# The residual rows go to DRAM as two fp16 parts, and the experts' slots are transposed as fp16

## The chip, the cores and the metric

The kernel runs on one core of one Trainium2 chip. The engines named here are PE (TensorE, matrix products and transposes; its weight loads have a row PEld of their own), DVE (VectorE), ACT (ScalarE), POOL (GpSimd) and SP (SyncE, which here only issues DMAs). They run their own instruction streams and meet at semaphores. The metric is the device time of one execution in microseconds, as the median of several runs.

## The reference

Two layers work on one sequence of 512 rows of 1024 numbers. Each layer has three sub-layers, and each ends in a layer norm over the residual sum.

```python
def grouped_moe(x, w_router, b_router, w_gate, w_up, w_down):
    xt = x.reshape(B * S, D)
    scores = jax.nn.softmax((xt @ w_router + b_router).astype(jnp.float32), axis=-1)
    ...                     # best group of experts, then the two best experts in it
    for e in range(N_EXPERTS):
        h = jax.nn.silu(xt @ w_gate[e]) * (xt @ w_up[e])
        y = y + gate[:, e:e + 1] * (h @ w_down[e])

def reference(x, mem, ...):
    for l in range(DEPTH):
        ...                 # gated linear attention and spatial gating, output projection
        x = layer_norm(DN_ALPHA * x + h, ln_g[l, 0], ln_b[l, 0])
        h = mem_xattn(x, mem, wq_x[l], wk_x[l], wv_x[l], wo_x[l])
        x = layer_norm(DN_ALPHA * x + h, ln_g[l, 1], ln_b[l, 1])
        h = grouped_moe(x, w_router, b_router, w_gate[l], w_up[l], w_down[l])
        x = layer_norm(DN_ALPHA * x + h, ln_g[l, 2], ln_b[l, 2])
```

The change touches the third sub-layer, the grouped mixture of 16 experts, and how the rows of `x` come to it. All inputs and the output are fp32.

## The kernel before

Every fp32 matrix product is made of three fp16 products. A number is scaled and split into a high fp16 part and a low part (the rest, rounded to fp16), and `mm3` (L167 to L170) adds high x high, high x low and low x high in PSUM. The scale of the weights is 256, of the activations 16 (`SX`). A split is one ACT copy for the high part, followed by one DVE pass (`SCALAR_TENSOR_TENSOR`: scale, subtract the high part) for the low part: `split_ps` (L172 to L174) does it out of PSUM.

**The weights** come in units of 128 x 2048 fp32 (1 MiB) through `Feed` (L66 to L157). `fill` (L90 to L100) lets SP issue a load (L98) whenever a raw slot is free. `pump` splits the oldest loaded unit: ACT makes `whi` (L124), DVE makes `wlo` (L129). With `aside`, DVE is left out: ACT makes `whi`, scales the raw unit in place (L126), and POOL subtracts (L127). When a unit is split its raw slot's kind is appended to the queue `rawfree`, and `fill` takes slots from the front of that queue, so slots go round in the order in which splits free them. Four slots of kind "b" exist throughout. During the experts there are more: seven of kind "x" (`RAW_X`), two of kind "y", and in layer 1 one called "mem". In the last layer the last eight units may take only slots "b" and "mem" (`xend`, L876). An odd expert's last down unit (not that of expert 15) is not split but read by PE as raw fp32 (L1216), and frees its slot only then.

**Ahead of the experts** the output projection of the cross-attention runs over four tiles of 128 rows (tiles 0 to 3, order at L1083 to L1119). Each tile gets its residual sum (L337), its statistics (L290, L293; ACT L294, L296) and its layer norm (L300, L303), all on DVE in place in the tile's fp32 rows `xr`. Tile 3 does the norm in two halves. Then `x3T` (L931) sends the tile's rows to the DRAM array `xd` by a DMA on ACT's queue (L932), PE transposes the tile, and `split_ps` makes the fp16 parts `x` for the router. `logits` (L937, DVE L942) and `route` (from L965, with L967) choose the experts. Between the tiles stand weight splits set aside to POOL, two in each layer and a third in layer 0 (L1096, L1101, L1110).

**The experts** have 96 slots each. POOL gathers an expert's rows from `xd` with an indirect DMA (L1137) into one of three fp32 buffers, three experts ahead. `dispatch` (L1152) turns a buffer: eight fp32 transposes on PE into two PSUM banks, and per bank one split into `xgh` (ACT L173) and `xgl` (DVE L174), 384 columns each. `gate_up` (L1169) makes both products; ACT's SiLU (L1177) and DVE's product (L1178) make `h`. `hid` (L1198) splits `h` (ACT L1203, DVE L1204). `down` (L1230) is the down projection; ACT L1234 takes it out of PSUM and POOL scatters the rows to DRAM (L1143). One turn of the loop (L1329 to L1340) is, in the order of the code: `gate_up(e)`, `dispatch(e + 1)`, `hid(e)`, one weight split, the gather of expert e + 3, and `down(e - 1)`; each engine follows that order in its own stream.

Of the kernel before, what the change touches and what calls it, by code (L numbers as in the profile page):

```python
# [36 lines left out]
RAW_B, HL_B = 4, 4  # L37
RAW_X, HL_X, RAW_Y = 7, 1, 2
YEND = 4
# [5 lines left out]
def trunk_kernel(ctx, tc, units, xT, x, memT, alow, wa2, b_a, gn_g, w_sT, b_s, slnT,  # L45
# [12 lines left out]
    def nm(s):  # L58
        cnt[0] += 1
        return f"{s}_{cnt[0]}"  # L60

    def ps():
        return psp.tile([P, 512], F32, tag="b", name=nm("ps"))


    class Feed:  # L66
        def __init__(self):
            self.items = []
            self.raw = {}
            self.hl = {}  # L70
            self.nload = 0
            self.nsplit = 0
            self.rawfree = deque("b" * RAW_B)
            self.hlfree = deque("b" * HL_B)
            self.px = self.px2 = self.ph = None
            self.limit = 1 << 30
# [13 lines left out]
        def fill(self, eng=nc.sync):  # L90
            while self.nload < min(len(self.items), self.limit):
                k = self.slot(self.rawfree, self.nload)
                if k is None:
                    return
                src, _, _, cols = self.items[self.nload]
                pl, b = {"b": (ring, RAW_B), "x": (self.px, RAW_X), "y": (self.px2, RAW_Y), "mem": (cp, 1)}[k]
                t = pl.tile([P, 2048], F32, tag="mem" if k == "mem" else "raw", bufs=b, name=nm("raw"))
                eng.dma_start(t[:, :cols], src)  # L98
                self.raw[self.nload] = (t, k)
                self.nload += 1  # L100
# [109 lines left out]

    xd = dram.tile([S, D], F32, name="xd")
    y2 = dram.tile([2 * S, D], F32, name="y2")
# [214 lines left out]
    for l in range(DEPTH):  # L427
# [441 lines left out]
        with ExitStack() as ex:  # L869
# [5 lines left out]
            fin = l == DEPTH - 1  # L875
            feed.xend = {"h": u["end"], "x": u["end"] - (8 if fin else 0), "y": u["end"] - (8 if fin else YEND), "mem": u["end"]}  # L876
            feed.limit = u["end"] + 4
# [53 lines left out]
            def x3T(t):  # L931
                nc.scalar.dma_start(xd[t * P:(t + 1) * P, :], xr[t])  # L932
                x3hl = (ep if t % 2 else x3p).tile([P, 2, KT, P], F16, tag="xg2" if t % 2 else "x3", name=nm("x3"))
                x3[t] = (x3hl[:, 0], x3hl[:, 1])
                transpose_x(t, *x3[t])

            def logits(t):  # L937
# [175 lines left out]
            rows = cp.tile([P, 4, D], F32, tag="actA", name=nm("rows"))  # L1113
            xg32 = [rows[:, 0], rows[:, 1]]
            for g in xg32:
                pool.memset(g, 0.0)
            idle(6, 0, 0)
            logits(NT - 1)
            xg32.append(ep.tile([P, D], F32, tag="xg2", name=nm("xg2")))  # L1119
            pool.memset(xg32[2], 0.0)  # L1120
            x3c.__exit__(None, None, None)
# [30 lines left out]
            def dispatch(e):  # L1152
                g = xg32[e % 3]
                xgh = ep.tile([P, KT, CAP], F16, tag="xgh", name=nm("xgh"))
                xgl = ep.tile([P, KT, CAP], F16, tag="xgl", name=nm("xgl"))
                for hf in range(2):
                    p = ps()
                    for j in range(4):
                        k = 4 * hf + j
                        pe.transpose(p[:, j * CAP:(j + 1) * CAP], g[:CAP, k * P:(k + 1) * P], ident[:CAP, :CAP])  # L1160
                    split_ps(xgh[:, 4 * hf:4 * hf + 4].rearrange("p k c -> p (k c)"),
                             xgl[:, 4 * hf:4 * hf + 4].rearrange("p k c -> p (k c)"), p[:, :4 * CAP], SX)
                E[e] = {"xg": (xgh, xgl)}

            def fetch(e):
                if e < NE:
                    gather(xg32[e % 3], idxT[:, e:e + 1])

# [90 lines left out]
            def overflow(fp):  # L1259
                most = nc.values_load(cnti[0:1, NE:NE + 1], min_val=0, max_val=S)  # L1260
                with tc.If(most > CAP):  # L1261
                    off = fp.tile([P, 1], F32, name="off")
                    dve.memset(off, 0.0)
                    with tc.For_i(CAP, S, CAP) as first:
                        dve.tensor_scalar(off, off, float(CAP), None, op0=OP.add)
                        with tc.For_i(0, NE, 1) as e:
                            ce = nc.values_load(cnti[0:1, bass.ds(e, 1)], min_val=0, max_val=S)
                            with tc.If(ce > first):
# [13 lines left out]
                                row_of(pg[:, 1:4], 1, ix[:, 1:2], gf)  # L1282
                                gather(xg32[0], ix[:CAP, 0:1])
                                xg = fp.tile([P, KT, CAP], F32, name="xg")
                                for hf in range(2):
                                    p = ps()
                                    for j in range(4):
                                        k = 4 * hf + j
                                        pe.transpose(p[:, j * CAP:(j + 1) * CAP], xg32[0][:CAP, k * P:(k + 1) * P],
                                                     ident[:CAP, :CAP])  # L1290
                                    act.activation(xg[:, 4 * hf:4 * hf + 4].rearrange("p k c -> p (k c)"),
                                                   p[:, :4 * CAP], AF.Copy)

# [60 lines left out]
            if not fin:  # L1354
                ln_open()
                load_ln(l, 2)
                down(NE - 1)
                pxc.__exit__(None, None, None)
                phc.__exit__(None, None, None)
                with tc.tile_pool(name=f"ovf{l}", bufs=1, reuse_waits="tile") as fp:  # L1360
                    overflow(fp)
            else:

                pxc.__exit__(None, None, None)
                ln_open()
# [164 lines left out]
```

## Time and profile before

| | |
|---|---|
| median of 3 runs | 1277.48 us (1275.62 to 1279.99) |
| the profiled execution's own time | 1278.14 us |
| its span (first to last instruction) | 1276.5 us |
| PE busy | 1172.9 us (92%), 11218 instructions |
| DVE busy | 909.9 us (71%), 1066 instructions |
| ACT busy | 711.1 us (56%), 810 instructions |
| POOL busy | 234.5 us (18%), 193 instructions |
| mean DMA rate over the span | 247 GB/s |

The table is of one profiled execution. The shares are means over stages that differ much: the two expert loops lie at about 385 to 615 us and 1010 to 1235 us, where the weights stream in at about 418 GB/s; ahead of each is the stage with the output projection, the layer norm and the routing. A row of a timeline gives the start of an instruction, its duration and, in brackets, how long its engine stood idle before it and which instruction's end released it.

### The profile page before, as it was taken

The numbers are of one execution on the slowest core, as the hardware profiler recorded it, in microseconds if no ns is written. First come the engines' busy times: TensorE is split into PE (matmuls) and PEld (weight loads), VectorE is DVE, ScalarE is ACT, GpSimd is POOL, SyncE is SP. The second block draws the span as 40 slices with busy tenths as digits, with TensorE's granted clock in tenths as the row PEclk, the third lists the DMA queues.
The fourth block names the chain that finished last, engine by engine and source line by source line (L and its number), as shares of the span: only waits on it lengthen the run. The fifth ranks groups of instructions, "written<-read, shape, count | busy, mean of one in ns | idle before, by whom it ended". The sixth has DMA issues, their size and how long they took to land. (4 is left out here: it accounts for less than half of the span.)

```text
span 1276.5 us, 26079 instructions
## 1 busy us (share of the span) xinstructions
PE 1172.9 (92%) x11218; PEld 760.2 (60%) x11219; DVE 909.9 (71%) x1066; ACT 711.1 (56%) x810; POOL 234.5 (18%) x193
## 2 busy tenths in 40 slices
PE   7999999999979999999859999999999899999973
PEld 4455456454557777777635545444644777777751
DVE  3255875378579999999474275673857789999977
ACT  3435334345448888888443444232633588888863
POOL 3002000000231223321250003000003222223214
PEclk9999999999989999999979999999998899999996
DMA  9412225227569999999671230154374799999964
GB/s 361 163 67 99 99 77 188 99 99 292 220 226 371 419 418 418 419 417 405 233 273 79 99 133 34 67 215 181 112 312 139 274 389 419 417 419 419 373 241 180
DMA packets 54941, 314.76 MB, mean 247 GB/s; under 512 B 9310, under 2 KB 9406, under 8 KB 22561
## 3 DMA queue, kind: packets, MB, share of 16 engines
q1 hardware_dynamic: 42096, 279.99, 56.0%
q0 software_dynamic: 11568, 28.83, 6.3%
q10 hardware_dynamic: 1152, 4.19, 0.8%
q8 instruction: 90, 1.47, 0.5%
q14 instruction: 35, 0.28, 0.1%
HBM read 302.80 MB, written 22.68 MB: 255 GB/s over the span
## 5 line engine op out<-in xcount | busy, mean ns | idle before, releaser
L129 DVE SCALAR_TENSOR_TENSOR wlo<-raw,whi 128x2048 f16<-128x2048 f32 (+1 forms) x234 | 521.8, 2277 | 101.0 <-ACT whi L124 100.6
L124 ACT ACTIVATE whi<-raw 128x2048 f16<-128x2048 f32 (+1 forms) x239 | 440.9, 1894 | 32.9 <-DMA raw<-in_units 16.7
L170 PE MATMUL ps<-xgh,wlo 128*128 128x96 f16 x2048 | 270.4, 207 | 12.9 <-DVE wlo L129 12.9
L168 PE MATMUL ps<-xgh,whi 128*128 128x96 f16 x2048 | 270.3, 207 | 4.7 <-ACTq L1261 4.2
L169 PE MATMUL ps<-xgl,whi 128*128 128x96 f16 x2048 | 270.2, 207 | 1.1 <-DVE xgl L174 1.1
L170 PEld LDWEIGHTS <-wlo 128*128 128x128 f16 x2400 | 236.4, 98 | 50.7 <-DVE wlo L129 16.7
L168 PEld LDWEIGHTS <-whi 128*128 128x128 f16 x2400 | 236.5, 99 | 39.1 <-issue 6.0
L169 PEld LDWEIGHTS <-whi 128*128 128x128 f16 x2400 | 236.4, 99 | 38.2 <-issue 8.5
L1143 POOL DMA_INDIRECT y<-rows,idxR x31 | 71.4, 2303 | 340.8 <-ACT rows L1234 331.1
L168 PE MATMUL ps<-whi,xT 128*128 128x512 f16 (+1 forms) x256 | 92.6, 362 | 8.4 <-ACT whi L124 7.1
L170 PE MATMUL ps<-whi,xT 128*128 128x512 f16 (+1 forms) x256 | 92.4, 361 | 2.2 <-DVE xT L174 2.2
L169 PE MATMUL ps<-wlo,xT 128*128 128x512 f16 (+1 forms) x256 | 92.5, 361 | 1.7 <-DVE wlo L129 1.7
L168 PE MATMUL ps<-whi,hhl 128*96 128x512 f16 x200 | 75.9, 379 | 1.1 <-ACT hhl L1203 1.1
L169 PE MATMUL ps<-wlo,hhl 128*96 128x512 f16 x200 | 75.7, 379 | 0.9 <-DVE wlo L129 0.9
L170 PE MATMUL ps<-whi,hhl 128*96 128x512 f16 x200 | 75.8, 379 | 0.0
L294 ACT ACTIVATE lnmv<-lnmv,c_lneps 128x1 f32<-128x1 f32 x16 | 4.7, 295 | 110.0 <-DVE lnmv L293 110.0
L1203 ACT ACTIVATE hhl<-h 128x384 f16<-128x384 f32 x32 | 16.7, 523 | 74.9 <-DVE h L1178 74.8
L1216 PE MATMUL ps<-raw,h 128*96 128x512 f32 x112 | 50.3, 592 | 0.0
L169 PE MATMUL ps<-x2T,whi 128*128 128x512 f16 x128 | 48.5, 379 | 1.0 <-DVE x2T L174 1.0
L169 PE MATMUL ps<-wlo,mx 128*128 128x512 f16 x128 | 48.5, 379 | 0.4 <-DVE wlo L129 0.3
L1137 POOL DMA_INDIRECT rows<-xd,idxT x22 | 40.4, 1838 | 45.6 <-DVE wlo L129 11.1
L168 PE MATMUL ps<-x2T,whi 128*128 128x512 f16 x128 | 48.5, 379 | 0.0
(309 smaller groups left out, 2052.2 us busy)
## 6 DMA issues: line engine op xcount, KB each, us to landing
raw<-in_units SPq DMA_DIRECT2D x249, 1024.0 KB
xd<-xr ACTq DMA_DIRECT2D x8, 512.0 KB
ya<-y SPq DMA_DIRECT2D x8, 512.0 KB
yb<-y SPq DMA_DIRECT2D x8, 512.0 KB
y<-zr SPq DMA_DIRECT2D x1, 4096.0 KB
lng<-in_ln_g POOLq DMA_DIRECT2D x6, 512.0 KB, 5.3
lnb<-in_ln_b POOLq DMA_DIRECT2D x6, 512.0 KB, 7.1
raw<-in_xT SPq DMA_DIRECT2D x4, 512.0 KB
```

Source lines behind the costliest of these rows:

```text
L124: act.activation(dest[0], t[:, :cols], AF.Copy, scale=scale)
L129: dve.scalar_tensor_tensor(dest[1], t[:, :cols], scale, dest[0], op0=OP.mult, op1=OP.subtract)
L168: pe.matmul(o, lh, rh, start=first, stop=False)
L169: pe.matmul(o, lh, rl, start=False, stop=False)
L170: pe.matmul(o, ll, rh, start=False, stop=last)
L294: act.activation(mvt[:, 2:3], mvt[:, 1:2], AF.Ln, bias=c_lneps, scale=(ISC * ISC if scaled else 1.0))
L1137: pool.indirect_dma_start(out=dst[:idx.shape[0], :], out_offset=None, in_=xd[:], in_offset=bass.IndirectOffsetOnAxis(ap=idx, axis=0), boun ...
L1143: i = pool.indirect_dma_start(out=y2[:], out_offset=bass.IndirectOffsetOnAxis(ap=idx, axis=0), in_=src[:CAP, :], in_offset=None, bounds_ch ...
L1203: act.activation(f2(hh), h32, AF.Copy)
L1216: pe.matmul(p[:CAP, :], E[e]["h"][:, f * CAP:(f + 1) * CAP], mv(w, f), start=(f == 0), stop=(f == 3))
```

## The change

The DRAM array `xd` held a row as 1024 fp32 numbers; now it holds 2048 fp16 numbers, the row's high part and its low part, both already scaled by 16. `x3T(t)` makes these parts itself: after the transposes and splits of the tile, one ACT copy (high) and one DVE pass (low) over 1024 columns of `xr[t]` into a tile `xs` (two of them, in a pool of their own). The DMA of tile t - 1 is now issued at the start of `x3T(t)`, the last after `logits(3)`. The gathers bring both parts with the same number of bytes a row. `dispatch` turns sixteen fp16 blocks instead of eight fp32 ones, eight into each PSUM bank, and takes each bank out with one plain ACT copy of 768 columns; DVE takes no part. The transposes need an fp16 identity (one DVE cast in each layer). One of the seven raw slots "x" is given up for the tiles `xs` and comes back as a slot "z" when these are no longer needed. The overflow path, for experts with more than 96 rows, is changed in the same manner; it stands in a branch.

```diff
-RAW_X, HL_X, RAW_Y = 7, 1, 2
+RAW_X, HL_X, RAW_Y, RAW_Z = 6, 1, 2, 1
...
-                pl, b = {"b": (ring, RAW_B), "x": (self.px, RAW_X), "y": (self.px2, RAW_Y), "mem": (cp, 1)}[k]
+                pl, b = {"b": (ring, RAW_B), "x": (self.px, RAW_X), "y": (self.px2, RAW_Y), "z": (self.pz, RAW_Z), "mem": (cp, 1)}[k]
...
-    xd = dram.tile([S, D], F32, name="xd")
+
+    xd = dram.tile([S, 2 * D], F16, name="xd")
...
-            feed.xend = {"h": u["end"], "x": u["end"] - (8 if fin else 0), "y": u["end"] - (8 if fin else YEND), "mem": u["end"]}
+            xsc = tc.tile_pool(name=f"xs{l}", bufs=1, reuse_waits="tile")
+            xsp = xsc.__enter__()
+            feed.xend = {"h": u["end"], "z": u["end"] - (8 if fin else 0), "x": u["end"] - (8 if fin else 0), "y": u["end"] - (8 if fin else YEND), "mem": u["end"]}
...
             def x3T(t):
-                nc.scalar.dma_start(xd[t * P:(t + 1) * P, :], xr[t])
+                if t > 0:
+                    put(t - 1)
...
                 transpose_x(t, *x3[t])
+                xs[t] = xsp.tile([P, 2, D], F16, tag="xs", bufs=2, name=nm("xs"))
+                act.activation(xs[t][:, 0], xr[t], AF.Copy, scale=SX)
+                dve.scalar_tensor_tensor(xs[t][:, 1], xr[t], SX, xs[t][:, 0], op0=OP.mult, op1=OP.subtract)
+
+            xs = {}
+
+            def put(t):
+                nc.scalar.dma_start(xd[t * P:(t + 1) * P, :], xs[t].rearrange("p a d -> p (a d)"))
...
-            xg32 = [rows[:, 0], rows[:, 1]]
-            for g in xg32:
+            half = lambda v: v.bitcast(F16)
+            xg16 = [half(rows[:, 0]), half(rows[:, 1])]
+            for g in (rows[:, 0], rows[:, 1]):
                 pool.memset(g, 0.0)
+            id16 = ep.tile([P, CAP], F16, name="id16")
+            dve.tensor_copy(id16, ident[:, :CAP])
             idle(6, 0, 0)
             logits(NT - 1)
-            xg32.append(ep.tile([P, D], F32, tag="xg2", name=nm("xg2")))
-            pool.memset(xg32[2], 0.0)
+            put(NT - 1)
+            xsc.__exit__(None, None, None)
+            pzc = tc.tile_pool(name=f"pz{l}", bufs=1, reuse_waits="tile")
+            feed.pz = pzc.__enter__()
+            feed.rawfree.extend("z" * RAW_Z)
+            xg2 = ep.tile([P, D], F32, tag="xg2", name=nm("xg2"))
+            pool.memset(xg2, 0.0)
+            xg16.append(half(xg2))
...
             def dispatch(e):
-                g = xg32[e % 3]
-                xgh = ep.tile([P, KT, CAP], F16, tag="xgh", name=nm("xgh"))
-                xgl = ep.tile([P, KT, CAP], F16, tag="xgl", name=nm("xgl"))
+                E[e] = {"xg": []}
                 for hf in range(2):
-                    p = ps()
-                    for j in range(4):
-                        k = 4 * hf + j
-                        pe.transpose(p[:, j * CAP:(j + 1) * CAP], g[:CAP, k * P:(k + 1) * P], ident[:CAP, :CAP])
-                    split_ps(xgh[:, 4 * hf:4 * hf + 4].rearrange("p k c -> p (k c)"),
-                             xgl[:, 4 * hf:4 * hf + 4].rearrange("p k c -> p (k c)"), p[:, :4 * CAP], SX)
-                E[e] = {"xg": (xgh, xgl)}
+                    x16 = ep.tile([P, KT, CAP], F16, tag="xg" + "hl"[hf], name=nm("x16"))
+                    p = turned(xg16[e % 3], hf)
+                    act.activation(x16.rearrange("p k c -> p (k c)"), p, AF.Copy)
+                    E[e]["xg"].append(x16)
+
+            def turned(g, hf):
+
+                p = ps().bitcast(F16)
+                for k in range(KT):
+                    c = hf * D + k * P
+                    pe.transpose(p[:, k * CAP:(k + 1) * CAP], g[:CAP, c:c + P], id16[:CAP, :])
+                return p[:, :KT * CAP]
```

The lines move by the added code: L300 becomes L301, L303 L304, L337 L338, the logits' L942 L954, L967 L979, L1178 L1202, L1203 L1227, L1204 L1228, L1234 L1258. L942 is now the low part of `xs`, L941 its high part.

**DVE, between tiles 2 and 3 of layer 0.** `xr_87` and `xr_88` are the rows of tiles 2 and 3, `x_324` and `x_325` the fp16 parts of the transposed tile 2. Before:

```order
L337 SCALAR_TENSOR_TENSOR xr_88<-xr_88,ps_2694 128x512
L290 BN_STATS lnst_2778<-xr_88 128x6
L174 SCALAR_TENSOR_TENSOR x_324_2815<-ps_2816,x_324_2815 128x512
L174 SCALAR_TENSOR_TENSOR x_324_2815<-ps_2823,x_324_2815 128x512
L337 SCALAR_TENSOR_TENSOR xr_88<-xr_88,ps_2789 128x512
L290 BN_STATS lnst_2778<-xr_88 128x6
```

Now:

```order
L338 SCALAR_TENSOR_TENSOR xr_88<-xr_88,ps_2697 128x512
L291 BN_STATS lnst_2784<-xr_88 128x6
L174 SCALAR_TENSOR_TENSOR x_325_2821<-ps_2822,x_325_2821 128x512
L174 SCALAR_TENSOR_TENSOR x_325_2821<-ps_2829,x_325_2821 128x512
L942 SCALAR_TENSOR_TENSOR xs_2836<-xr_87,xs_2836 128x1024
L338 SCALAR_TENSOR_TENSOR xr_88<-xr_88,ps_2795 128x512
L291 BN_STATS lnst_2784<-xr_88 128x6
```

The pass L942 on tile 2's rows has come between tile 2's splits and the second half of tile 3's residual sum; tiles 0, 1 and 3 have the same pass behind their splits.

**DVE, one expert in layer 0's loop.** `h` is the expert's hidden product, `xgl` the low part of the next expert's rows, `hhl` the low part of `h`. Before:

```order
L129 SCALAR_TENSOR_TENSOR wlo_3785<-raw_3148,whi_3784 128x2048
L1178 SCALAR_TENSOR_TENSOR h_408_3673<-ps_3681,h_408_3673 128x384
L174 SCALAR_TENSOR_TENSOR xgl_3889<-ps_3890,xgh_3888 128x384
L174 SCALAR_TENSOR_TENSOR xgl_3889<-ps_3897,xgh_3888 128x384
L1204 TENSOR_TENSOR hhl_3904<-h_408_3673,hhl_3904 128x384
L129 SCALAR_TENSOR_TENSOR wlo_3908<-raw_3205,whi_3907 128x2048
L129 SCALAR_TENSOR_TENSOR wlo_3918<-raw_3259,whi_3917 128x2048
```

Now:

```order
L129 SCALAR_TENSOR_TENSOR wlo_3824<-raw_3175,whi_3823 128x2048
L1202 SCALAR_TENSOR_TENSOR h_412_3712<-ps_3720,h_412_3712 128x384
L1228 TENSOR_TENSOR hhl_3949<-h_412_3712,hhl_3949 128x384
L129 SCALAR_TENSOR_TENSOR wlo_3953<-raw_3232,whi_3952 128x2048
L129 SCALAR_TENSOR_TENSOR wlo_3963<-raw_3286,whi_3962 128x2048
```

The two passes for `xgl` between the product and the split of `h` are gone; the weight splits around them stand as they did.

**SP, the last loads of layer 1's weights.** Each row is a load of one unit; in brackets what SP waits for ahead of it: earlier DMAs (DMAHW), and the split (DVE) or the matrix product (PE) that frees the slot. Before:

```order
L98 DMA raw_14387<-in_units 128x2048 [waits DMAHW1_49,DVE_49]
L98 DMA raw_14397<-in_units 128x2048 [waits DMAHW2_49,DVE_49]
L98 DMA raw_14653<-in_units 128x2048 [waits DMAHW4_49,DMAHW3_49,DVE_49]
L98 DMA raw_14677<-in_units 128x2048 [waits DMAHW6_49,DVE_49]
L98 DMA raw_14755<-in_units 128x2048 [waits DMAHW5_49,DMAHW1_49,DVE_49]
L98 DMA raw_14809<-in_units 128x2048 [waits DMAHW2_49,DVE_49]
L98 DMA raw_14932<-in_units 128x2048 [waits DMAHW7_49,DMAHW3_49,DVE_49]
L98 DMA raw_14939<-in_units 128x2048 [waits DMAHW0_49,PE_49]
```

Now:

```order
L98 DMA raw_14491<-in_units 128x2048 [waits DMAHW1_49,DVE_49]
L98 DMA raw_14620<-in_units 128x2048 [waits DMAHW2_49,DVE_49]
L98 DMA raw_14630<-in_units 128x2048 [waits DMAHW3_49,DVE_49]
L98 DMA raw_14892<-in_units 128x2048 [waits DMAHW4_49,DVE_49]
L98 DMA raw_14916<-in_units 128x2048 [waits DMAHW6_49,DMAHW5_49,DVE_49]
L98 DMA raw_14994<-in_units 128x2048 [waits DMAHW1_49,DVE_49]
L98 DMA raw_15048<-in_units 128x2048 [waits DMAHW7_49,DMAHW2_49,DVE_49]
L98 DMA raw_15177<-in_units 128x2048 [waits DMAHW3_49,DMAHW0_49,DVE_49]
```

Before, the last load takes the slot of the raw unit that PE reads; now all eight take slots that a split frees.

## Rows read from the trace of the kernel before

**Rows 1.** Page, its first line (the span) and the row of its forty slices with the busy share of the core's 16 DMA engines in tenths.

```profile
span 1276.5 us, 26079 instructions
...
DMA  9412225227569999999671230154374799999964
```

**Rows 2.** Busy time of each engine in one stretch of layer 0's expert loop, 30.46 us long: from one scatter of an even expert to the next. Columns: the window, its length, PE, PEld, DVE, ACT and POOL busy us (instructions), granted clock, DMA share, GB/s.

```profile
430.46:460.92 30.46, 29.38 (x444) 23.45 (x444) 28.21 (x20) 25.39 (x24) 8.92 (x4) 1.00 1.02 418
```

**Rows 3.** Timeline of DVE in that stretch. Columns: start us, duration us (of a run of x instructions, together), engine, line, operation, out<-in, shape; in brackets the idle time before it and what released it.

```profile
442.13 0.55 DVE L1178 SCALAR_TENSOR_TENSOR h<-ps,h 128x384 f32<-128x384 f32 x1
442.60 1.01 DVE L174 SCALAR_TENSOR_TENSOR xgl<-ps,xgh 128x384 f16<-128x384 f32 x2
443.53 0.55 DVE L1204 TENSOR_TENSOR hhl<-h,hhl 128x384 f16<-128x384 f32 x1
445.07 4.49 DVE L129 SCALAR_TENSOR_TENSOR wlo<-raw,whi 128x2048 f16<-128x2048 f32 x2 [0.99 <-ACT whi L124]
```

**Rows 4.** Timeline of ACT in the same stretch.

```profile
439.30 0.85 ACT L173 ACTIVATE xgh<-ps 128x384 f16<-128x384 f32 x2
442.71 0.52 ACT L1203 ACTIVATE hhl<-h 128x384 f16<-128x384 f32 x1 [2.56 <-DVE h L1178]
443.14 3.69 ACT L124 ACTIVATE whi<-raw 128x2048 f16<-128x2048 f32 x2
```

**Rows 5.** Groups of instructions over the whole span, shapes kept apart. Columns: line, engine, operation, out<-in, shape, count | busy us together, mean ns of one | idle time before them and what ended most of it.

```profile
...
L124 ACT ACTIVATE whi<-raw 128x2048 f16<-128x2048 f32 x237 | 438.8, 1901 | 32.3 <-DMA raw<-in_units 16.2 <-PE ps L170 15.8 <-issue 0.2
...
L174 DVE SCALAR_TENSOR_TENSOR xgl<-ps,xgh 128x384 f16<-128x384 f32 x64 | 32.6, 548 | 8.0 <-ACT xgh L173 7.7
...
L173 ACT ACTIVATE xgh<-ps 128x384 f16<-128x384 f32 x64 | 27.6, 482 | 33.1 <-PE ps L1160 32.8
...
L129 DVE SCALAR_TENSOR_TENSOR xT<-raw,xT 128x1024 f16<-128x1024 f32 x4 | 4.9, 1225 | 9.3 <-ACT xT L124 9.3
```

**Rows 6.** Timeline of DVE ahead of layer 0's expert loop: the end of the output projection with its layer norms (L337, L300, L303), the splits of the transposed tiles (L174), and the first steps of the routing (L942, L967).

```profile
333.47 0.68 DVE L337 SCALAR_TENSOR_TENSOR xr<-xr,ps 128x512 f32<-128x512 f32 x1
...
336.53 0.69 DVE L337 SCALAR_TENSOR_TENSOR xr<-xr,ps 128x512 f32<-128x512 f32 x1 [1.66 <-PE ps L170]
...
343.16 1.29 DVE L174 SCALAR_TENSOR_TENSOR x<-ps,x 128x512 f16<-128x512 f32 x2 [0.92 <-ACT x L173]
344.37 0.68 DVE L337 SCALAR_TENSOR_TENSOR xr<-xr,ps 128x512 f32<-128x512 f32 x1
...
346.05 1.96 DVE L300 SCALAR_TENSOR_TENSOR xr<-xr,lnmv,lng 128x512 f32<-128x512 f32 x2
347.94 1.40 DVE L303 SCALAR_TENSOR_TENSOR xr<-xr,lnmv,lnb 128x512 f32<-128x512 f32 x2
...
352.73 0.17 DVE L942 SCALAR_TENSOR_TENSOR scs<-ps,scs 128x16 f32<-128x16 f32 x1 [0.51 <-PE ps L170]
...
353.19 1.46 DVE L967 TENSOR_TENSOR scs<-scs,cr 128x64 f32<-128x64 f32 x1
```

**Rows 7.** Timeline of POOL in the same stretch: the subtractions of the weight splits that are set aside.

```profile
331.88 4.08 POOL L127 TENSOR_TENSOR wlo<-raw,whi 128x2048 f16<-128x2048 f32 x1 [33.77 <-ACT raw L126]
342.73 4.08 POOL L127 TENSOR_TENSOR wlo<-raw,whi 128x2048 f16<-128x2048 f32 x1 [6.76 <-ACT raw L126]
350.50 4.07 POOL L127 TENSOR_TENSOR wlo<-raw,whi 128x2048 f16<-128x2048 f32 x1 [3.69 <-ACT raw L126]
```

**Rows 8.** Timeline of ACT at the first expert of layer 0.

```profile
383.36 0.87 ACT L173 ACTIVATE xgh<-ps 128x384 f16<-128x384 f32 x2 [0.70 <-PE ps L1160]
384.34 0.52 ACT L1203 ACTIVATE hhl<-h 128x384 f16<-128x384 f32 x1
```

**Rows 9.** All instructions of one line over the span: count, duration in ns as minimum/median/maximum, first and last start, and the forms.

```profile
L300 DVE SCALAR_TENSOR_TENSOR xr<-xr,lnmv,lng x20: 741/1285/1309, 154.0 to 973.1; 128x1024 f32<-128x1024 f32 x12, 128x512 f32<-128x512 f32 x8
...
L967 DVE TENSOR_TENSOR scs<-scs,cr x2: 226/840/1455, 353.2 to 978.5; 128x64 f32<-128x64 f32 x2
...
L686 POOL TENSOR_TENSOR sq<-o x8: 1029/1032/2537, 111.1 to 773.9; 128x512 f32<-128x512 f32 x8
```

**Rows 10.** Timelines of DVE, POOL and ACT in the same stage of layer 1, in that order.

```profile
970.16 0.68 DVE L337 SCALAR_TENSOR_TENSOR xr<-xr,ps 128x512 f32<-128x512 f32 x1
...
971.84 1.97 DVE L300 SCALAR_TENSOR_TENSOR xr<-xr,lnmv,lng 128x512 f32<-128x512 f32 x2
...
984.16 0.36 DVE L1001 SCALAR_TENSOR_TENSOR scr<-ps,ch 128x64 f32<-128x64 f32 x2 [1.65 <-PE ps L993]
...
968.52 4.07 POOL L127 TENSOR_TENSOR wlo<-raw,whi 128x2048 f16<-128x2048 f32 x1 [6.72 <-ACT raw L126]
...
1008.54 0.53 ACT L1203 ACTIVATE hhl<-h 128x384 f16<-128x384 f32 x1
```

**Rows 11.** Timeline of ACT at the last expert of layer 1, and the row of SP's queue (SPq: DMA issues) at 1223.90.

```profile
1229.09 1.91 ACT L124 ACTIVATE whi<-raw 128x2048 f16<-128x2048 f32 x1 [0.30 <-DMA raw<-in_units]
1233.38 1.91 ACT L124 ACTIVATE whi<-raw 128x2048 f16<-128x2048 f32 x1 [2.38 <-DMA raw<-in_units]
1235.20 1.24 ACT L1234 ACTIVATE rows<-ps,gall 96x512 f32<-96x512 f32 x2
...
1223.90 0.81 SPq L98 DMA_DIRECT2D raw<-in_units  x2
```

**Rows 12.** Busy time of each engine from 355 to 365 us, columns as in rows 2.

```profile
355.00:365.00 10.00, 7.67 (x43) 3.35 (x41) 7.88 (x31) 1.74 (x1) 3.84 (x4) 0.83 0.56 211
```

More of the change, by code (lines that the diff above doesn't have):

```diff
@@ L74, in __init__ @@
             self.hlfree = deque("b" * HL_B)
-            self.px = self.px2 = self.ph = None
+            self.px = self.px2 = self.pz = self.ph = None
             self.limit = 1 << 30
@@ L1152, in dispatch @@
             def dispatch(e):
-                g = xg32[e % 3]
-                xgh = ep.tile([P, KT, CAP], F16, tag="xgh", name=nm("xgh"))
-                xgl = ep.tile([P, KT, CAP], F16, tag="xgl", name=nm("xgl"))
+                E[e] = {"xg": []}
                 for hf in range(2):
-                    p = ps()
-                    for j in range(4):
-                        k = 4 * hf + j
-                        pe.transpose(p[:, j * CAP:(j + 1) * CAP], g[:CAP, k * P:(k + 1) * P], ident[:CAP, :CAP])
-                    split_ps(xgh[:, 4 * hf:4 * hf + 4].rearrange("p k c -> p (k c)"),
-                             xgl[:, 4 * hf:4 * hf + 4].rearrange("p k c -> p (k c)"), p[:, :4 * CAP], SX)
-                E[e] = {"xg": (xgh, xgl)}
+                    x16 = ep.tile([P, KT, CAP], F16, tag="xg" + "hl"[hf], name=nm("x16"))
[8 more added lines that the diff above has]
+                return p[:, :KT * CAP]
             def fetch(e):
                 if e < NE:
-                    gather(xg32[e % 3], idxT[:, e:e + 1])
+                    gather(xg16[e % 3], idxT[:, e:e + 1])
             def gate_up(e, mid=None):
@@ L1282, in overflow @@
                                 row_of(pg[:, 1:4], 1, ix[:, 1:2], gf)
-                                gather(xg32[0], ix[:CAP, 0:1])
+                                gather(xg16[0], ix[:CAP, 0:1])
                                 xg = fp.tile([P, KT, CAP], F32, name="xg")
[L1285 to L1292, printed above, removed]
+                                xg_ = xg.rearrange("p k c -> p (k c)")
+                                act.activation(xg_, turned(xg16[0], 0), AF.Copy, scale=1.0 / SX)
+                                dve.scalar_tensor_tensor(xg_, turned(xg16[0], 1), 1.0 / SX, xg_,
+                                                         op0=OP.mult, op1=OP.add)
                                 def wload(j):
@@ L1357, in trunk_kernel @@
                 down(NE - 1)
+                pzc.__exit__(None, None, None)
                 pxc.__exit__(None, None, None)
@@ L1362, in trunk_kernel @@
             else:
+                pzc.__exit__(None, None, None)
                 pxc.__exit__(None, None, None)
```

## The prediction

> **What bounds the kernel now.** Read first the page for span and slices, then the expert loops by stretches of one pair of experts, then DVE and ACT inside a pair, then the layer-norm and routing stage ahead of the loop, and the last expert at the end.
>
> The span is 1276.5 us of a profiled execution of 1278.14 us, 1.64 us around it; the median of the runs is 1277.48, 0.7 lower. I sum against 1278.14. Inside the expert loops the DMA row shows nines [rows 1], and a pair of experts takes 30.46 us at 418 GB/s with DVE busy 28.21 and ACT 25.39 [rows 2]. It looks as if DVE, the engine the change relieves, were the bound. The order inside a pair says more: DVE's product h (L1178) ends at 442.68; ACT's hhl waits for exactly that (2.56 us idle) and starts at 442.71; ACT's next split whi follows at 443.14 and lasts until 445.04; DVE, idle for 0.99 us, starts its wlo at 445.07 [rows 3, 4]. From the end of h to the next wlo are 2.39 us which ACT sets. The two xgl passes (442.60 to 443.61) and L1204 stand inside them. Then DVE works a backlog of wlo passes up to the next h, so the period is this chain plus the wlo passes.
>
> Ahead of the loop DVE makes layer norm, splits and routing one after the other, while POOL runs three (layer 0) or two (layer 1) passes of 4.08 us each for the weight splits that are set aside [rows 7, 10]. Some DVE instructions there are far too long: the first L300 of tile 3 (two halves 1.96 us, where L303 of the same size takes 1.40), L967 with 1.46 where its other execution took 0.226 [rows 6, 9]. Both started under a POOL pass and ended just behind it (342.73 + 4.08 = 346.81; 350.50 + 4.07 = 354.57, against 354.65). Both read two tensors from SBUF. L337 and L174, which read PSUM and one SBUF tensor, kept their time under the same passes [rows 6].
>
> **The change part by part.**
>
> *Expert loop: xgl goes from DVE.* Two passes of 548 ns, 64 in all [rows 5], off an engine that then waits for ACT anyhow: the 0.99 us of idle time become about 1.9. I count 0. Bounds: 0 and 0.93 x 30 = 28 us faster.
>
> *Expert loop: ACT copies 2 x 768 columns in place of 2 x 384.* 482 ns for 384 and 1901 for 2048 columns [rows 5] give 0.85 ns a column and 0.81 us for 768, so 0.67 us more for the two back to back. They stand before hhl, where ACT idles 2.56 us [rows 4]: hidden. The trace has no ACT read of f16 from PSUM; were one copy as long as the 2048-column pass, 3.8 us would meet 0.85 + 2.56 = 3.41 of room, and each expert would be 0.4 longer. Only the first expert of a layer has no such idle time: hhl starts at 384.34, 0.11 behind the end of L173, and 1008.54 in layer 1 [rows 8, 10]. There the longer copies cost 0.5 and 0.75 us.
>
> *PE: 16 f16 transposes in place of 8 f32*, before the down projection, with DVE and not PE in the chain: 0. The same bytes cross DMA (4,096 a row both ways): 0. A wait of SP for the last write of the slots before loads z and y go out: what queues behind it are loads, and over the whole span ACT's splits waited only 16.2 us for loads [rows 5]: 0.
>
> *Tiles: a new f32 to f16 split.* Per tile one ACT copy and one DVE pass over 1024 columns (1225 ns, the nearest row by shape, [rows 5]), and DVE's stands behind the splits x and before the next layer-norm step. This pass reads xr and xs, both in SBUF. Under tiles 1 and 2 (and 3 in layer 0) it is issued while POOL's pass runs, since both POOL's and this tile's work start when ACT's L126 is done. So I price it as L300 is: it ends 1.04 us behind POOL's end (1.23 less the 0.2 by which a held pass is shorter, from L300 and L967).
>
> Layer 0, tile 1: POOL ends 335.96, the pass 337.0. The next L337 started 333.47 and now 336.92; its second follows 1.44 later, at 338.36, where PE let it start at 336.53 [rows 6, 7]: +1.8. Tile 2: POOL's pass moves by 1.8 too and ends 348.6, the new one 349.65, so the L337 of 344.37 starts 349.57: +5.2. Tile 3: ACT's chain carries 5.2 on; POOL ends 359.77, the pass 360.8, the cast to id16 0.2 later; then L942, L966 and L967 (now 0.23, since POOL is idle) end 361.6, where L967 ended 354.65: +6.95. With 0.5 for the first dispatch: **+7.4**.
>
> [...]
>
> Layer 1: the same up to the second L337 of tile 3: 970.16 becomes 975.3, +5.2. The first L300 there loses its 0.57 of waiting (1.97 against 1.40), since POOL is done: +4.6. The new pass of tile 3 has no POOL pass beside it; its 1.2 + 0.2 lie beside PE's warm-up matmuls, for which L1001 waited 1.65 us [rows 10]. With 0.75 for the first dispatch: **+5.4**. The first tile's pass is covered in both layers by a wait for PE ahead of the next residual sum; if not, 1.2 each.
>
> *The end of layer 1: which loads find a slot.* The last eight loads may take only the four b slots and mem. Slots go round in the order in which splits free them, and six x slots at first in place of seven turn this round by one. Followed by hand through Feed, the last load no longer takes the slot of the raw unit that PE reads (the PE wait in the row of SP's order), and the last but one goes out two splits earlier. Before, the last two went out together at 1223.90; ACT waited 2.38 us for the last, split it at 1233.38, and evacuated the down projection at 1235.20 [rows 11]. Now only the last goes out then; it lands where the other did, about 1229.0. ACT splits both from 1228.8 to 1232.5, and L1234 starts then: **-2.7**. Bounds: 0 and -4.3 (1233.3 to 1229.0).
>
> Sum: 7.4 + 5.4 - 2.7 = +10.1; 1278.1 + 10.1 = **1288.2 us**.
>
> **The rivals.**
>
> *A: the new pass is not held by POOL.* For it: no L129, the pass of the same operand types, stands under a POOL pass in the trace. Against it: L300 and L967, and POOL's L686, which took 2537 in place of 1029 ns where an L129 was running [rows 9]. Then tile 1 is covered by PE, tile 2 costs 1.4, tile 3 hides behind L967's own wait in layer 0: 1.4 + 0.5, and in layer 1 1.4 - 0.57 + 0.75; with -2.7 that is about +0.8: **1279**, not slower by what can be measured. It decides when a pass issued under POOL's takes 1.2 us.
>
> *B: the loop gets shorter.* If wlo could run past h, 0.93 us an expert would go. Against it: rows 3 and 4, and the loads: 12 units are 12.58 MB, 30.1 us at 418 GB/s, 0.36 less than a pair takes; beyond that only buffered units can be used up, some 2 to 4 of 2.5 us a layer, an estimate. 10.1 - 5 - 5 to 10: about **1276**.
>
> *C: ACT becomes the bound* by the upper price of an f16 copy: 0.4 x 31 = 12 more: **1300**.
>
> *D: the loads at the end land no earlier*, because scatter and layer-norm loads share the DMA then: **1291**.
>
> **Chances.** Forecast 0.60, D 0.15, A 0.10, B 0.08, C 0.07. What this kernel's measurement can tell from no change is about 0.3%, 3.8 us. Faster by more takes half of B and a little of A: 0.05. Within 0.3%: the rest of A and B: 0.14. Slower: 0.81. The forecast's own range is 1284 to 1293: +2.7 without the gain at the end, +1 for the cast, up to 2 for PE, which now waits some 3 us longer before tile 3 and whose granted clock was 0.83 from 355 to 365 us already [rows 12], and the other way -1.6 at the end and 2 for overlaps between tiles that I put one behind the other. For 8 in 10, A is taken in below; C is left out: 1278 to 1294.
>
> **What the next profile shows.** Right: pairs of 30.46 us with DVE idle near 1.9 before wlo; hhl still released by h; new DVE passes of tiles 1 and 2 of over 2 us under POOL's L127; the routing's L967 some 7 us later in layer 0 and near 5 in layer 1; ACT's wait for the last load gone. Wrong: new passes of 1.2 us there (A), a shorter period (B), hhl released by ACT's own copies in the steady loop (C), the wait for the last load still over 2 us (D).

## The result and the profile after

The changed kernel takes 1296.63 us (median of 4 runs, 1293.99 to 1298.14) against 1277.74 for the kernel before on the same chips: a ratio of 1.0145 (95% interval 1.0131 to 1.0159), 18.9 us slower. The forecast was 1288, its range 1278 to 1294. The profiled execution took 1297.92 us, 19.8 more than that of before. The page's first line and PE's busy time:

```profile
span 1296.2 us, 26529 instructions
...
PE 1176.4 (91%) x11474; PEld 764.0 (59%) x11475; DVE 899.2 (69%) x1012; ACT 738.7 (57%) x818; POOL 242.2 (19%) x193
```

Set beside each other, the same instruction's start in the two traces gives the delay up to that place. The table takes the differences between neighbouring places; tiles 1 and 2 count as done when the residual sum L337 behind them starts.

| place (start before, us) | delay there | gained or lost on the way | forecast |
|---|---|---|---|
| L337 at the head of layer 0's stage (304.76) | +1.69 | +1.7 | 0 |
| tile 1 done (340.83) | +3.42 | +1.7 | +1.8 |
| tile 2 done (344.37) | +6.80 | +3.4 | +3.4 |
| L967 ends (354.65) | +10.00 | +3.2 | +1.75 |
| first h of layer 0 (383.76) | +12.35 | +2.35 | +0.5 |
| last h of layer 0 (608.72) | +12.35 | 0 | 0 |
| a residual sum L337 of layer 1's first sub-layer (809.85) | +14.80 | +2.45 | 0 |
| second h of layer 1 (1019.72) | +20.41 | +5.6 | +5.4 |
| last weight's evacuation (1235.20) | +17.47 | -2.9 | -2.7 |
| end of the span (1276.5) | +19.7 | +2.2 | 0 |

**The loop did not move.** One pair of experts, 12.35 us later than in [rows 2] (columns as there):

```profile
442.81:473.27 30.46, 29.39 (x460) 23.46 (x460) 26.54 (x16) 26.68 (x24) 8.92 (x4) 1.00 1.01 416
```

It is 30.46 us again, with DVE busy 26.54 in place of 28.21. DVE (first fence) and ACT (second) inside it, to be read against [rows 3, 4]:

```profile
454.48 0.55 DVE L1202 SCALAR_TENSOR_TENSOR h<-ps,h 128x384 f32<-128x384 f32 x1
455.62 0.56 DVE L1228 TENSOR_TENSOR hhl<-h,hhl 128x384 f16<-128x384 f32 x1 [0.59 <-ACT hhl L1227]
457.42 4.49 DVE L129 SCALAR_TENSOR_TENSOR wlo<-raw,whi 128x2048 f16<-128x2048 f32 x2 [1.24 <-ACT whi L124]
```

```profile
451.65 1.49 ACT L1178 ACTIVATE x<-ps 128x768 f16<-128x768 f16 x2
455.06 0.52 ACT L1227 ACTIVATE hhl<-h 128x384 f16<-128x384 f32 x1 [1.92 <-DVE h L1202]
455.50 3.69 ACT L124 ACTIVATE whi<-raw 128x2048 f16<-128x2048 f32 x2
```

DVE's two idle times are now 0.59 and 1.24 us, 1.83 together where before there were 0.99: the two xgl passes became idle time. ACT's two f16 copies of 768 columns take 1.49 us together, and hhl still waits for h, 1.92 us in place of 2.56.

**The stage ahead of it did.** DVE between tiles 1 and 3 of layer 0, then POOL:

```profile
335.38 3.34 DVE L942 SCALAR_TENSOR_TENSOR xs<-xr,xs 128x1024 f16<-128x1024 f32 x1
338.65 0.67 DVE L338 SCALAR_TENSOR_TENSOR xr<-xr,ps 128x512 f32<-128x512 f32 x1
...
347.96 3.28 DVE L942 SCALAR_TENSOR_TENSOR xs<-xr,xs 128x1024 f16<-128x1024 f32 x1
351.17 0.68 DVE L338 SCALAR_TENSOR_TENSOR xr<-xr,ps 128x512 f32<-128x512 f32 x1
...
359.16 3.29 DVE L942 SCALAR_TENSOR_TENSOR xs<-xr,xs 128x1024 f16<-128x1024 f32 x1
362.37 1.73 DVE L1131 CAST id<-ident 128x96 f16<-128x96 f32 x1
362.49 1.61 DVE L954 SCALAR_TENSOR_TENSOR scs<-ps,scs 128x16 f32<-128x16 f32 x1
...
364.42 0.23 DVE L979 TENSOR_TENSOR scs<-scs,cr 128x64 f32<-128x64 f32 x1
```

```profile
333.57 4.08 POOL L127 TENSOR_TENSOR wlo<-raw,whi 128x2048 f16<-128x2048 f32 x1 [33.77 <-ACT raw L126]
346.09 4.07 POOL L127 TENSOR_TENSOR wlo<-raw,whi 128x2048 f16<-128x2048 f32 x1 [8.44 <-ACT raw L126]
357.29 4.08 POOL L127 TENSOR_TENSOR wlo<-raw,whi 128x2048 f16<-128x2048 f32 x1 [7.13 <-ACT raw L126]
361.30 1.84 POOL L1129 MEMSET rows<- 128x1024 f32 x2
363.09 0.96 POOL L1140 MEMSET xg<- 128x1024 f32 x1
```

Each of these three new passes L942 was issued under POOL's L127, took 3.28 to 3.34 us where tile 0's took 1.22, and ended 1.07 to 1.08 us behind it (346.09 + 4.07 = 350.16; 347.96 + 3.28 = 351.24). The next residual sum L338 starts at that moment, as [rows 6, 7] had suggested for L300. L979, the old L967, takes 0.23 now in place of 1.46: its wait has gone to L942. The cast to id16 took 1.73 us, to the end of the last memset (363.09 + 0.96 = 364.05), and L954 stood behind it.

From the first gather's issue to its first use, before and after, as two stretches (columns as in [rows 2], the last is GB/s):

```profile
363.40:370.07 6.67, 1.14 (x6) 0.30 (x4) 4.11 (x17) 0.00 (x0) 4.97 (x4) 0.91 0.64 219
```

```profile
373.50:382.14 8.64, 1.15 (x6) 0.33 (x5) 4.12 (x17) 0.00 (x0) 4.97 (x4) 0.79 0.96 347
```

8.64 us in place of 6.67, while DMA moved 347 GB/s in place of 219. What the loads on SP's queue waited for between 340 and 385 us (us in total, times, longest):

```profile
SPq L98 <- DMA xd<-xs: 7.1, 1, 7.1
```

SP waited 7.1 us for the last write of the new rows. The two loads behind it left at 369.04 and 369.47, 4.0 us or a little more ahead of the gather; before, the last two left at 354.59 and 355.11, over 8 us ahead of it.

At the end of layer 1 ACT no longer waits for the last load [rows 11]: the two splits follow at once, then the evacuation.

```profile
1249.07 3.71 ACT L124 ACTIVATE whi<-raw 128x2048 f16<-128x2048 f32 x2
1252.67 1.26 ACT L1258 ACTIVATE rows<-ps,gall 96x512 f32<-96x512 f32 x2
```

### The profile page after: what moved, and what is told of

Its sections match the earlier page's. It is cut to its first block, busy times and chain, and to the rows that moved or that the text cites. A ratio compares the mean times of both kernels' runs of the same rounds, so it can differ in the third digit from the quotient of the medians.

```text
span 1296.2 us, 26529 instructions
## 1 busy us (share of the span) xinstructions
PE 1176.4 (91%) x11474; PEld 764.0 (59%) x11475; DVE 899.2 (69%) x1012; ACT 738.7 (57%) x818; POOL 242.2 (19%) x193
## 5 line engine op out<-in xcount | busy, mean ns | idle before, releaser
L129 DVE SCALAR_TENSOR_TENSOR wlo<-raw,whi 128x2048 f16<-128x2048 f32 (+1 forms) x234 | 521.7, 2277 | 105.9 <-ACT whi L124 104.4
L170 PE MATMUL ps<-x,wlo 128*128 128x96 f16 x2048 | 269.9, 207 | 13.8 <-DVE wlo L129 13.8
L168 PE MATMUL ps<-x,whi 128*128 128x96 f16 x2048 | 269.7, 207 | 4.8 <-DVEq L1285 3.6
L169 PE MATMUL ps<-x,whi 128*128 128x96 f16 x2048 | 269.5, 207 | 1.0 <-ACT x L1178 1.0
L1178 ACT ACTIVATE x<-ps 128x768 f16<-128x768 f16 x64 | 47.9, 802 | 31.6 <-PE ps L1186 31.6
L1227 ACT ACTIVATE hhl<-h 128x384 f16<-128x384 f32 x32 | 16.7, 523 | 58.5 <-DVE h L1202 57.7
L169 PE MATMUL ps<-x2T,whi 128*128 128x512 f16 x128 | 48.5, 379 | 1.0 <-DVE x2T L174 1.0
```

Of the source, the lines that this page charges most:

```text
L129: dve.scalar_tensor_tensor(dest[1], t[:, :cols], scale, dest[0], op0=OP.mult, op1=OP.subtract)
L168: pe.matmul(o, lh, rh, start=first, stop=False)
L169: pe.matmul(o, lh, rl, start=False, stop=False)
L170: pe.matmul(o, ll, rh, start=False, stop=last)
L1178: act.activation(x16.rearrange("p k c -> p (k c)"), p, AF.Copy)
L1227: act.activation(f2(hh), h32, AF.Copy)
```

## The experiments

**The changed kernel once more (again).**

> The changed kernel once more, nothing edited. In its first profile 1.69 us were lost already at 141 us of the span, ahead of the first changed instruction, and 2.45 us between the two expert stages (620 to 810 us), both beside stretches in which the granted TensorE clock stood at 0.50. Theory 'the clock falls differently in each execution': this profile loses other amounts at these two places, by some 2 us each, and the median lies within 2 us of 1296.6. Rival 'they come with the change': 1.7 and 2.4 us again at the same places.

1294.38 us (1292.96 to 1295.08), ratio 1.0127 (1.0101 to 1.0154). At the first place 1.69 us again, at the second 1.34 in place of 2.45. In the profiles of the kernels below, the delay ahead of the first changed instruction was 0.1 (id_early) to 2.6 us (aside_on_dve) where the new split of the rows is in, and 0.2 to 0.6 in the four without it; what came on between the expert stages was -1.2 (before_hid) to 3.8 (turn_only). Inconclusive: the second amount changes from execution to execution and does not follow the edits. The first came out the same twice, as the rival said, and is larger with the change in all profiles but one; why is open. The clock stands beside the second: the stretch of 85 us behind layer 0's experts, before and after, with a mean granted clock of 0.88 and 0.82 (the third column from the end):

```profile
615.00:700.00 85.00, 63.54 (x427) 44.22 (x425) 46.28 (x46) 33.24 (x50) 24.37 (x27) 0.88 0.52 192
```

```profile
627.00:712.00 85.00, 62.43 (x412) 43.81 (x411) 45.39 (x45) 31.41 (x48) 24.39 (x27) 0.82 0.52 193
```

**The split ahead of POOL's work (cut_early).** The split of tiles 1 to 3, ACT's copy and DVE's pass, is moved, nothing else. Tile 2:

```diff
             op_.ln(2)
+            cut(2)
             op_.ln0(3)
...
             feed.pump(1, True)
             x3T(2)
```

> The new split of tiles 1 to 3 stands right behind the tile's layer norm, ahead of the weight split that is set aside to POOL; tile 0 and all else as changed. Theory 'the pass is held by POOL': L942 of tiles 1 to 3 takes 1.2 us in place of 3.3, tile 1 costs nothing, tiles 2 and 3 some 1.1 us each (ACT's copy ahead of its other work), so 4 to 5 us come back in layer 0 and 4 in layer 1: about 1288. Rival 'the pass is dear by itself or by its place in DVE's row': passes of 3.3 us, 1296. Rival 'the dispatch or the gathers carry the loss': passes shorter, but the time above 1293.

1292.34 us, ratio 1.0115 (1.0083 to 1.0148), not 1288. Layer 1's stage cost 2.5 us to the second expert in place of 5.6 (4.3 in again), but layer 0's still 10.3 to its first h. DVE's new passes of tiles 2 and 3 and the cast, then POOL:

```profile
343.22 1.23 DVE L946 SCALAR_TENSOR_TENSOR xs<-xr,xs 128x1024 f16<-128x1024 f32 x1 [1.12 <-ACT xs L945]
...
354.74 1.23 DVE L946 SCALAR_TENSOR_TENSOR xs<-xr,xs 128x1024 f16<-128x1024 f32 x1 [1.12 <-ACT xs L945]
...
360.17 5.15 DVE L1138 CAST id<-ident 128x96 f16<-128x96 f32 x1
```

```profile
358.52 4.06 POOL L127 TENSOR_TENSOR wlo<-raw,whi 128x2048 f16<-128x2048 f32 x1 [7.45 <-ACT raw L126]
362.52 1.84 POOL L1136 MEMSET rows<- 128x1024 f32 x2
364.31 0.95 POOL L1147 MEMSET xg<- 128x1024 f32 x1
```

The passes take 1.23 us: the hold is real and is gone. But the cast, now issued under POOL's L127, waited for that and for the three memsets behind it, 5.15 us, until 365.32, where the last memset ended at 365.26; that is where most of layer 0's gain went. The pass and the cast did not wait for the same things. In the changed kernel's first profile the pass of tile 3 ended at 362.45, 1.08 us behind POOL's subtraction (361.37) and under the memsets of 361.30 (1.84 us for two); the cast behind it took 1.73 us, to the end of the last memset. No run shows why the two differ.

**The dispatch alone (turn_only).** `xd` gets the router's fp16 parts; no `xs`, seven x slots:

```diff
-                nc.scalar.dma_start(xd[t * P:(t + 1) * P, :], xs[t].rearrange("p a d -> p (a d)"))
+                nc.scalar.dma_start(xd[t * P:(t + 1) * P, :], x3f[t])
```

> The dispatch part alone: gathers of fp16 rows, sixteen fp16 transposes and two ACT copies of 768 columns an expert, but no split of the residual rows. What goes to DRAM in its place are the router's fp16 parts of the same tile (transposed, so the experts get the wrong numbers), same bytes; seven x slots and no z as before; the identity is cast at the start of the stage. Theory: 30.46 us a pair as before and 0.4 to 0.8 us at the first expert of each layer: 1279 (1277 to 1281). Rival 'the f16 copies or gathers are dear': 1285 or more.

1278.53 us, ratio 1.0005 (0.9993 to 1.0017): fp16 gathers, sixteen transposes and long copies cost nothing that can be measured in the whole time, and DVE's relief brings nothing. 30.47 us a pair, 0.55 lost at layer 0's first expert; the first gather is used after 6.9 us.

**The slots alone (slots_only).** The kernel before with `RAW_X = 6` and a slot z after `logits(3)`.

> The kernel before with only the slots changed: six x slots and one z that comes after the logits, no new split, fp32 rows. Theory 'the order of the last loads gives 2 to 3 us': L1234 of expert 14 starts 2.7 to 2.9 us earlier, about 1 of it given back in the tail's loads, 1275.5. Rival 'nothing at the end, as scatter and layer-norm loads share the DMA': 1277.7. If the z load meets the first gather of layer 0 here too, that gather lands 1 to 2 us later and the two cancel: 1277.

1276.77 us, ratio 0.9990 (0.9978 to 1.0003). The evacuation at the end came 3.0 us earlier, the end of the span 1.0: 2.0 are given back in the tail. The last scatter left 3.0 us earlier (1233.72 against 1236.72), the first read of its rows only 0.7 (1240.45 against 1241.11). The order of the slots does what the forecast said; what it is worth can't be told from no change. No gather was late.

**The cast at the start of the stage (id_early).** `id16` is made ahead of `x3T(0)`.

> The changed kernel with the cast of the identity moved to the start of the stage, nothing else. With the split moved the cast had stood 5.15 us under POOL's subtraction and memsets, at its changed place 0.84 to 1.73 under memsets. Theory 'the cast is held by POOL's memsets in layer 0': the logits of tile 3 end 0.8 to 1.7 us earlier there, nothing in layer 1 (0.2): 1294. Rival 'the cast is cheap, it was late for another reason': same times at the routing, 1295.5.

1291.90 us, ratio 1.0117 (1.0094 to 1.0140). Up to the end of the routing's L979 layer 0 lost 6.7 us from the stage's head, in place of 8.3 (first profile) and 7.4 (again): the cast had cost 0.7 to 1.6. The passes still took 3.28.

**Slot z given out later (z_late).**

```diff
-            feed.rawfree.extend("z" * RAW_Z)     # behind logits(3)
...
             feed.rawfree.append("y")
             feed.fill(pool)
+            feed.rawfree.extend("z" * RAW_Z)
```

> The changed kernel with slot z given out behind the loads that follow the first two gathers, nothing else. In the changed kernel layer 0's first gather was used 8.6 us after its issue, before the change 6.7, and the DMAs moved 347 GB/s in that stretch in place of 219. Theory 'the loads that waited for the last write of the residual rows meet the first gather': 6.7 to 7 us again, 1.5 to 2 us less in layer 0; the end of layer 1 may lose its 2.9 us if the order of the slots turns back: 1293.5 to 1296. Rival 'rows of two fp16 parts are slower to gather': 8.6 us stay.

1292.86 us, ratio 1.0123 (1.0105 to 1.0141). The first gather's stretch:

```profile
372.39:379.26 6.87, 1.14 (x7) 0.33 (x4) 4.11 (x17) 0.00 (x0) 4.96 (x4) 0.84 0.92 332
```

6.87 us again, and layer 0 lost 8.6 us from the stage's head to its first h in place of 10.66. The DMAs move 332 GB/s here too, so their sum does not decide it, and the fp16 rows do not either (6.9 us in turn_only). The late gather repeats in the kernels that left the order here as it was: 8.6 us in the first profile, 9.0 in again and id_early, 9.8 in hid_on_dve. That z's load alone makes it late is not shown: change_mended below, with z late, has 8.0 us, and aside_on_dve, with z early and the last of the waiting loads 3.7 us ahead of the gather, has 7.0. The 2.9 us at the end stayed.

**All three (all_three).** Cast early, z late, and the split moved as in cut_early, with DVE's pass one step behind ACT's copy.

> Cast early, slot z late, and the new split of tiles 1 to 3 ahead of POOL's work, ACT's copy right behind the layer norm and DVE's pass one step later, so that DVE does not wait for the copy. Theory 'holding by POOL, 5 us a layer and more, and the collision are the loss': L942 1.2 us everywhere, layer 0's first dispatch 3 to 4 us later than before the change, layer 1's 2 to 3, 2 back at the end: 1281 (1279 to 1285). Rival 'more work on ACT and DVE ahead of the loop is the loss wherever it stands': above 1288.

1289.48 us, ratio 1.0091 (1.0075 to 1.0108): the theory's 1281 is missed, the rival's figure came. ACT at tile 2:

```profile
342.42 1.06 ACT L948 ACTIVATE xs<-xr 128x1024 f16<-128x1024 f32 x1 [2.10 <-DVE xr L304]
343.39 1.89 ACT L124 ACTIVATE whi<-raw 128x2048 f16<-128x2048 f32 x1
```

ACT's copy now stands ahead of its weight split and waits 2.10 us for the layer norm; before, that split ran in this time. Copy and wait push POOL's pass, the transposed splits and the next residual sum back by 3.1 us, and at tile 3 by 3.7 more. The wait had changed the engine: from DVE behind POOL to ACT behind DVE.

**The set-aside splits on DVE (aside_on_dve).** The change's order is untouched, POOL has nothing to subtract:

```diff
-            feed.pump(1, True)
+            feed.pump(1)
```

(at all three places)

> The changed kernel, all splits where the change put them, but the weight splits that were set aside to POOL are made by DVE (2.28 us each, ACT's copy in place of 1.91 us left out). Theory 'the pass is held by POOL': L942 of tiles 1 to 3 takes 1.2 us at the very place where it took 3.3; the cast takes 0.2 or waits for memsets alone; DVE's own extra passes eat part of it, 1290 to 1293. Rival 'what holds the pass is its place in DVE's row or its operands': 3.3 us stay, and the time is above 1297.

1282.73 us, ratio 1.0036 (1.0020 to 1.0051): 12 to 14 us of the loss are gone, more than expected. DVE at tile 2 and the cast:

```profile
344.80 2.27 DVE L129 SCALAR_TENSOR_TENSOR wlo<-raw,whi 128x2048 f16<-128x2048 f32 x1
346.99 1.28 DVE L174 SCALAR_TENSOR_TENSOR x<-ps,x 128x512 f16<-128x512 f32 x2
348.19 1.22 DVE L942 SCALAR_TENSOR_TENSOR xs<-xr,xs 128x1024 f16<-128x1024 f32 x1
...
358.36 0.52 DVE L1131 CAST id<-ident 128x96 f16<-128x96 f32 x1
```

L942 takes 1.22 us at the very place where it took 3.28. DVE makes an additional L129 of 2.27 us and is still earlier, since ACT has lost its L126 of 1.91 us and the transposed splits no longer wait for that. Layer 0's stage costs 1.6 us to the second expert, layer 1's 2.1.

**The high part of h on DVE (hid_on_dve, in the changed kernel; before_hid, in the kernel before).**

```diff
-                act.activation(f2(hh), h32, AF.Copy)
+                dve.tensor_copy(f2(hh), h32)
```

> The changed kernel with the high part of h made by DVE in place of ACT (L1227's copy), nothing else, so that ACT's weight splits no longer stand behind DVE's product. Theory 'h, ACT's copy, ACT's next split set the period': the pair of 30.46 us falls to 29.6 to 30.1, where DMA or PE take over, 8 to 12 us less in all: 1285. Rival 'PE (29.4 of 30.46 us busy) or the loads set it': 30.46 stays within 0.1, 1295.

> The kernel before with the high part of h made by DVE in place of ACT, nothing else: xgl still on DVE. The same edit brought the changed kernel from 30.46 to 28.89 us a pair until the loads ended the gain. Theory 'the chain over ACT was the bound, not DVE's work': DVE has 28.21 busy plus 0.7, so some 29.2 to 29.6 us a pair until the loads limit it, 6 to 9 us less: 1270. Rival 'the gain needs the 1 us an expert that the change took off DVE': 30.2 us or more a pair, 1275 to 1277.

1283.75 us (ratio 1.0052, 1.0032 to 1.0071) and 1272.24 us (0.9971, 0.9948 to 0.9994). In the changed kernel a pair early in layer 0 and one late in it, and DVE in the first:

```profile
438.30:467.20 28.90, 28.90 (x462) 23.38 (x461) 27.18 (x18) 26.08 (x22) 8.92 (x4) 1.00 1.02 418
573.16:605.20 32.04, 30.06 (x464) 23.56 (x462) 27.54 (x19) 26.42 (x22) 3.68 (x2) 1.00 1.01 418
```

```profile
451.02 0.55 DVE L1202 SCALAR_TENSOR_TENSOR h<-ps,h 128x384 f32<-128x384 f32 x1
451.60 0.36 DVE L1227 CAST hhl<-h 128x384 f16<-128x384 f32 x1
452.00 0.56 DVE L1228 TENSOR_TENSOR hhl<-h,hhl 128x384 f16<-128x384 f32 x1
452.47 4.49 DVE L129 SCALAR_TENSOR_TENSOR wlo<-raw,whi 128x2048 f16<-128x2048 f32 x2
```

The chain is gone at this expert: the next wlo follows the split of h at once. At the pair's other expert DVE still waits 1.24 us for ACT's whi, but the pair takes 28.90 us with PE busy all of it. Later the buffered units are used up and the loads set 32.0 us, still at 418 GB/s. The kernel before, with xgl still on DVE, gets as far:

```profile
439.49:468.22 28.73, 28.73 (x445) 23.30 (x444) 28.66 (x22) 24.64 (x22) 9.19 (x4) 1.00 1.01 418
```

28.73 us, DVE busy all but 0.07. So what bound the loop was ACT standing between two DVE steps, not DVE's work, and before_hid's rival falls: the microsecond that the change takes off DVE is not needed for it. The whole time fell by 5 us, less than the 6 to 9 expected: late in layer 0 two of the pairs took 32.8 and 33.8 us.

**Both of these on the kernel before (before_hid_slots).**

> The kernel before with the high part of h on DVE and the change's slots (six x and a z), fp32 rows as before. If the two gains add: 1 us below the run with h alone, about 1269. If the loads bind the end of the loop once h is faster, the order of the last slots may decide more or nothing: 1267 to 1272.

1268.35 us (1267.42 to 1269.89), ratio 0.9928 (0.9911 to 0.9946): 9 us faster than the kernel before and 26 to 28 faster than the change. It is the fastest of all.

**The change with everything mended (change_mended).** aside_on_dve, id_early, z_late and hid_on_dve together.

> The changed kernel with all that was found: weight splits on DVE in place of POOL ahead of the loop, cast early, slot z late, high part of h on DVE. Theory: the change's own cost ahead of the loops (about 5.4 us over the kernel before) stays but for 0.5, and the faster loop gives 8 to 9 back, as it did for the kernel before: 1273 to 1275. That would be 5 us or more above the kernel before with the same two edits of slots and h (1268.35). Rival 'with h on DVE the 1 us an expert that the change takes off DVE begins to count': 1269 or less.

1273.59 us, ratio 0.9967 (0.9953 to 0.9980). As the theory said, 5 us above before_hid_slots, and with 28.89 us a pair no faster in the loop (28.74 there): the dispatch saves nothing here either. In its profile layer 0 lost 2.4 us from the stage's head to its first h, 1.4 of them at the gather (8.04 us in place of 6.67), and layer 1 1.9 to its second. That the extra pass and copy per tile make up all the rest of the 5 us is argued, not shown.

## Why the forecast was right and wrong

Slower was right; 1296.63 us lies above the range that ended at 1294. The largest cost, the held passes, was there as described. Too small were the cast's wait, the delayed loads (put at nothing) and what comes back behind the last evacuation.

- **The loop (0): right**, in size and in reason. The idle time before wlo and hhl grew to 1.83 us, the pair stayed at 30.46, turn_only cost nothing, and taking ACT out of the chain, not DVE's work, shortened the pair. Rival B had the limit right: with h on DVE the loads end such a gain (32.0 us a pair).
- **The f16 copies: right.** 802 ns by the page's mean against 0.81; rival C falls.
- **The held passes: right to 0.1 us**, tiles 1 and 2 in both layers (1.7 and 3.4). cut_early and aside_on_dve show the hold from two sides; rival A falls.
- **Tile 3 of layer 0 (+1.75): mis-sized, 3.2.** "The cast to id16 0.2 later" was the step that failed. The "+1 for the cast" in the forecast's range has no row of before behind it, and no run shows that figure: the cast met two memsets and took 1.73, in z_late and hid_on_dve too, one in again (0.84), a subtraction and three in cut_early (5.15). With the cast made earlier (id_early) tile 3 cost 1.6, the forecast's 1.75 less its 0.2.
- **SP's wait ahead of z and y (0): the step that failed outright, 1.9 us.** I asked only when the splits behind these loads come, not what the delayed loads run into. SP waited 7.1 us for the last write, the loads left close ahead of the first gather, and it was used 2.0 us later (up to 3.1 in other executions). z_late agrees; change_mended and aside_on_dve show that z's place alone does not decide it, so which load it is stays open.
- **The slots at the end (-2.7): right there (-2.9), wrong in the sum.** 2.2 us were given back between there and the last store, 2.0 in slots_only. Rival D had nearly the price, not its cause: the loads did land earlier, and in slots_only the time went between the last scatter and the first read of its rows.
- **First experts (0.5 and 0.75): right** (0.4 beside the gather in layer 0, 0.7 in layer 1). In layer 1 the pass of tile 3 hid 0.95 of its 1.4 us behind PE's warm-up work; the forecast had hidden all of it. That layer's stage as a whole, 5.6 us, took 4.3 in again, so its agreement with 5.4 is in part luck.
- **What no term held:** 1.69 us ahead of any change and 2.45 between the layers in this execution, with no cause shown. I had put up to 2 us for PE's clock into the forecast's own range and only for the stage ahead of the experts. The four misses, 1.5, 1.9, 2.2 and 4.1 us, make up the 9.7 between the forecast and the profile.

## What to carry to other kernels

Ask which engine arrives last before work is moved off one: DVE was 93% busy here, and yet 1.67 us less of it in a pair left the pair at 30.46 us, while ACT's copy between two of DVE's steps, given to DVE, made it 28.90 early in layer 0. The added DVE pass with two SBUF inputs was priced by what POOL did at that time (3.3 us), not by its own length (1.2). Where it was moved, look at what its feeder has queued: in all_three ACT waited 2.10 us for the layer norm ahead of its own weight split, and the next residual sum came 3.1 us later. When an edit delays loads, look at what runs where they land now.

## What was not expected

- Weight splits given to POOL to relieve DVE cost more than they saved in the changed kernel, where DVE has a two-input pass beside them: taking them back gained 12 to 14 us, though DVE has 2.3 us more to do at each place. Whether the kernel before would gain as well was not tried.
- In cut_early the cast on DVE did not get in between POOL's instructions that followed each other: 5.15 us behind one subtraction and three memsets, where layer 1's cast took 0.20. In again it waited for one memset alone, 0.84 us.
- Layer 0's first gather was used 6.9 to 9.8 us after its issue in the kernels with the change, and 6.87 against 8.64 us came at nearly the same DMA rate (332 against 347 GB/s).
